# Three modulation vectors of layer 0: from GpSimd products with ScalarE row sums to TensorE products on four column groups

## The chip, the core and the metric

One core of a Trainium2 chip. The core has TensorE (PE in the rows; its weight loads are PEld), VectorE (DVE), ScalarE (ACT), GpSimd (POOL) and SyncE (SP), which issues nearly all DMAs. Each engine works off its own queue in order and waits on semaphores for the others. The metric is the device time of one execution in microseconds (us); lower is better.

## The reference, cut to what matters

Two layers of a backbone over 512 tokens (256 of context, 256 latent) of 1024 features: layer 0 is a bidirectional Mamba-2 mixer and a SwiGLU feed-forward, layer 1 a bidirectional RWKV-7 mixer and a mixture of experts. Both are modulated by vectors made from a conditioning vector, `c` for the latent tokens and `c_ctx` for the context:

```python
m  = split(silu(c)     @ mod_w[i] + mod_b[i], 6)
mc = split(silu(c_ctx) @ mod_w[i] + mod_b[i], 6)
h  = rmsnorm(x, norm1_g[i]) * (1 + m[1]) + m[0]
x  = x + m[2] * mixer(h)
h2 = rmsnorm(x, norm2_g[i]) * (1 + m[4]) + m[3]
x  = x + m[5] * ffn(h2)
```

So each layer has six parts, each a product of a 1024 x 1024 matrix with two vectors. Parts 0 and 1 of layer 0 are wanted first, part 2 at the end of its mixer, parts 4 and 3 at its second norm, part 5 in its feed-forward. All is float32.

## The kernel before, in words

The activations lie feature-major, 128 features on the partitions and 512 tokens along a row. A large product takes a weight tile of 1024 x 256 in two loads of 512 KB (`wraw`, L190 to L198, from a ring of five tiles), which ScalarE rounds to a leading part (`whi`, L206) and VectorE, or GpSimd for the tiles of z, subtracts to a trailing part (`wlo`, L207). TensorE then does three matmuls per block (L212 to L214) into accumulator banks (`acc`, three of them; `misc`, two, is for everything small).

There are two ways to make a modulation vector.

`mod_products(n)` (L236) makes 256 entries of it, two feature tiles, and is used for parts 0 and 1 in the prologue (n from 0 to 7, L350). It loads a 1024 x 256 tile of `mod_w`, clears an accumulator bank on VectorE (L240), and for each of the 8 blocks of 128 rows multiplies by the 2 columns of silu(c) with the 2 columns as the weights and 256 columns as the moving data (L243). Block k goes to partitions 32 (k mod 4), so that four column groups of the array each sum two blocks. ScalarE copies the bank to SBUF (`modev`, L245), two matmuls with a 0/1 matrix `sel` add the four groups up and turn them onto the partitions (L248), and VectorE adds the bias (L250).

`mod_sums(l, part, js, eng)` (L253) makes one feature tile of 128 entries per step from the transposed weights: it loads 512 KB, multiplies them by a broadcast silu(c) (`scb`) and takes the row sums. Where `eng` is VectorE, a product and its row sum are one instruction (L261), one for each of the two vectors. Where it is GpSimd, GpSimd multiplies (L264) into `mprod`, of which there is one, or in place, and ScalarE copies the product over itself with a row sum (L265). Eight steps make a part, and VectorE adds the bias at the next call (L269).

`mod_queue` (L272) strings the parts together, layer 0's 2, 4, 3 (GpSimd and ScalarE) and 5 (VectorE), then layer 1's six (VectorE): 80 steps. `mod_some(n)` (L275) takes the next n steps. It is called at the head of a weight product: two steps in `x_products` (L491, 8 calls), one in `gate_z` (L573, 8 calls), so that parts 2, 4 and 3 are done by the end of the mixer; two at each of the four output products (L615); none in the first four feed-forward tiles, two in most others (L648, L661); what is left goes ahead of the RWKV part (L679).

The mixer of layer 0 runs over four groups of heads, each in two halves. `inputs` makes B and C, `x_products` the projection of x, `mix` convolves (`conv`: four tap sums per tile, L459), builds chunk states (GpSimd's products L520, matmuls L523) and per head a decay mask by exponentials on ScalarE (L546), multiplied by C times B on VectorE (L548) and by x on TensorE (L551). `gate_z` projects z and gates, with a running sum of squares on GpSimd (L303). Before it stands a chain of small VectorE operations on the time steps (L404 to L440), which ends in transposes on TensorE (L439).

The order on each queue isn't the program's: it is planned at build time by a list scheduler with its own estimates of durations, which takes the instructions by their place in the program and fills gaps with later ones. On the chip each queue then keeps that order.

Of the kernel before, what the change touches and what calls it, by code (L numbers as in the profile page):

```python
# [10 lines left out]
F32 = mybir.dt.float32  # L11
# [3 lines left out]
AF = mybir.ActivationFunctionType  # L15
# [50 lines left out]
def prepare(inp):  # L66
# [4 lines left out]
    a["w_mod"] = _tiles(g["mod_w"][0], [[(256 * n, 256 * n + 256)] for n in range(8)])  # L71
# [47 lines left out]
    # of the even heads' products (0) the first rows, of the odd heads' (1) the last take the minus sign  # L119
# [18 lines left out]
def tile_backbone(ctx: ExitStack, tc: tile.TileContext, T, out: bass.AP, dbg=None, stop=99):  # L138
# [50 lines left out]
    def wraw(src):  # L189
        """one weight tile, four rows blocks at a time: the blocks' access patterns"""  # L190
        kt, n = src.shape[1], src.shape[2]
        out = []
        for k in range(0, kt, 4):
            m = min(4, kt - k)
            w = wp.tile([128, 4, 256], F32, name="wraw", bufs=5)
            SY.dma_start(w[:, :m, :n], src[:, k:k + m, :])
            out.append(w[:, :m, :n])
        return out  # L198
# [17 lines left out]
    def accumulate(o, w, x_at, k0, nk):  # L216
        """add the products of the weight tile's row blocks k0, k0 + 1, ... of nk; four blocks for one
        column tile at a time, so that the next bank is asked for late"""
        c = o[0].shape[0]
        for q in range(0, len(w), 8):  # L220
            for m in range(len(o)):
                for i, (hi, lo) in enumerate(w[q:q + 8]):
                    k = k0 + q + i
                    mm3(o[m], hi[:, c * m:c * m + c], lo[:, c * m:c * m + c], *x_at(k), k == 0, k == nk - 1)

# [10 lines left out]
    def mod_products(n):  # L236
        """the first two parts of layer 0, wanted first: products of the tensor engine"""
# [6 lines left out]
        ev = xp.tile([128, 256], F32, name="modev", bufs=2)  # L244
# [8 lines left out]
    def mod_sums(l, part, js, eng):  # L253
        """the other parts: row sums of the transposed weights times silu(c)"""
        for n in range(8 * part, 8 * part + 8):
            w = wp.tile([128, 4, 256], F32, name="wraw", bufs=5).rearrange("p a b -> p (a b)")
            SY.dma_start(w, T["w_modT"][l, n])
            for j in js:
                t = w if j == js[-1] else rowp.tile([128, D], F32, name="mprod", bufs=1)
                if eng is V:  # L260
                    V.scalar_tensor_tensor(t, w, 0.5, scb[:, j, :], op0=ALU.mult, op1=ALU.mult,  # L261
                                           accum_out=mods[l][:, n, j:j + 1])
                else:
                    G.tensor_mul(t, w, scb[:, j, :])  # L264
                    S.activation(t, t, AF.Copy, scale=0.5, accum_out=mods[l][:, n, j:j + 1])  # L265
# [5 lines left out]
    MOD_ENG = {(0, 2): G, (0, 4): G, (0, 3): G, (0, 5): V}  # L271
    mod_queue = (x for l, part in ((0, 2), (0, 4), (0, 3), (0, 5), (1, 1), (1, 0), (1, 2), (1, 4), (1, 3), (1, 5))  # L272
                 for x in mod_sums(l, part, (0, 1) if l == 0 or part < 2 else (0,), MOD_ENG.get((l, part), V)))

# [7 lines left out]
    # token halves: ctx columns 0..255 take modulation 1, latent columns 256..511 modulation 0  # L282
    HALF = ((slice(0, 256), 1), (slice(256, 512), 0))

    class Squares:
        """running sum of squares over feature tiles, and from it 1/rms of each token on every partition"""
# [5 lines left out]
        def add(self, src, late=False):  # L292
            """late: summed by the tensor engine, with the rows"""
# [30 lines left out]
    def norm_mod(pool, l, norm, rb, X, hi, lo):  # L324
        """adaLN: hi + lo = X * rb * g * (1 + scale) + shift"""
# [31 lines left out]
    # =====================================================================  # L357
    # layer 0 mixer: bidirectional Mamba-2
    # =====================================================================
# [4 lines left out]
    with ExitStack() as es:  # L364
# [11 lines left out]
        def project(w, n=2, cols=128):  # L376
            """products of n column tiles of a weight tile"""
# [5 lines left out]
        # -- time steps: softplus, decay sums in both directions  # L383
# [23 lines left out]
        # log1p(e) = 2 atanh(e / (2 + e)), series in the square of the quotient (at most 1/9)  # L407
# [41 lines left out]
        def conv(o, m, dst):  # L449
            """centred depthwise convolution of one feature tile, per sequence, and silu;  # L450
            half the convolution is taken, h, and silu(2 h) = h (tanh(h) + 1)"""
# [18 lines left out]
        def inputs(g):  # L470
            """the group's B and C, feature-major; B token-major; products of C and B in each chunk"""
# [18 lines left out]
        def x_products(g, s):  # L490
            mod_some(2)  # L491
            return project(wsplit(T["w_mb"][5 * g + 1 + 2 * s], XE))

        def mix(g, s, px, bf, cf, btm, cb):
            """convolution, states and sums of four heads in both directions"""
# [16 lines left out]
            # states entering each chunk  # L512
# [59 lines left out]
        def gate_z(g, s):  # L572
            mod_some(1)  # L573
# [28 lines left out]
    # gated norm and output projection; the norm's factor is applied after the product  # L602
# [29 lines left out]
    # =====================================================================  # L632
    mark("ffn")
    # layer 0 feed-forward: SwiGLU, its hidden features in two halves
    # =====================================================================
    with ExitStack() as es:
# [8 lines left out]
        for hf in range(2):  # L645
            hid = []
            for n in range(NH):
                mod_some(0 if hf == 0 and n < 4 else 2)  # L648
# [26 lines left out]
    # =====================================================================  # L675
    # layer 1 mixer: bidirectional RWKV-7, in chunks of 64 tokens
    # =====================================================================
# [14 lines left out]
    # a block's rows of its second and of its first half  # L692
# [12 lines left out]
    # sigmoid(z) = (1 + tanh(z / 2)) / 2, and 1 + (sigmoid(z) - 1) k_a likewise  # L705
# [7 lines left out]
    # states of each direction, and the solutions of a chunk: the even heads' tile holds zeros in  # L713
    # the odd heads' rows and the other way round
# [5 lines left out]
    def weave(*gens):  # L720
        """emit the pieces of several instruction streams in turn"""
# [16 lines left out]
    def later(dst, src, after):  # L738
        """a load that leaves the queue to the transfers before after is there"""
# [3 lines left out]
    class Weights:  # L743
        """weight tiles in the order of their use: loaded ahead by halves, split by pairs of row blocks"""

        def __init__(self, pool, srcs, nraw, nsp, after=None, eng=(V, G), raw=None, part=None, first=SY):
            """raw, part: where the weights and their parts wait, when not in pool"""
# [36 lines left out]
    def products(W, units, x_at, nk=8):  # L784
        """units of nk feature tiles each: (columns, token-major, done). Both column tiles of a unit
        share a bank. x_at(unit, k) gives the two parts of the unit's k-th feature tile"""
# [24 lines left out]
    def normed(up, j):  # L811
        """modulated norm of one token sequence (0: ctx, 1: latent), feature-major, a zero at either end"""
        mj = 1 - j
        # each tile of the latent stream gives way to the difference of its neighbours
# [16 lines left out]
    def unit_keys(F, hT, rs, kbank):  # L831
        """the keys times the reciprocal of each head's norm, rs"""
# [7 lines left out]
    def features(up, F, names, MB, nraw, nsp, base, normed_all=None, vx=None, xs=None, later_x=None, raw=None, part=None, tail=None, eng=(V, G)):  # L840
        """projections of one sequence, feature-major except the values"""
# [75 lines left out]
        def value(n):  # L917
            def done(o):
                # rows of the head's opposite half
# [31 lines left out]
        def x_at(u, k):  # L951
# [4 lines left out]
            # the next mixture's tile takes the place of the last but one  # L956
# [17 lines left out]
    class Unit:  # L974
        """half of the heads of one token sequence (0: ctx, 1: latent), both directions"""
# [14 lines left out]
    def stage(tp, rp, F, un, d, l2, nb, bks, tags, ready):  # L990
        """everything of one direction of a unit that needs no state, but for the inverses"""
# [54 lines left out]
        def operands(c, dd, slot):  # L1046
# [6 lines left out]
            # the even heads' tile holds zeros in the odd heads' rows and the other way round  # L1053
# [12 lines left out]
        def grams(c, BK, slot):  # L1066
            """products of the earlier tokens (rows) with the later (columns), masked"""
# [44 lines left out]
    def spin(o, x):  # L1112
        """products that nothing reads, between the short ones: the tensor engine's clock falls to half when it waits"""
        PE.matmul(o[:, :x.shape[1] * x.shape[2]], ident, x, start=True, stop=True)

    def invert(tp, un, zbank, slots={}, warm=(0, 0)):
        """inverses of the unit triangular blocks: by substitution in 16 by 16 blocks, two per partition,
        then joined by products, first in blocks of 32, then of 64. In between blocks on the partitions
        turn into rows on the partitions. Of the second direction the substitution sees the transposes.
        slots: the tiles to take the place of, with their shapes; warm: after how many columns spin runs,  # L1120
        in either set of products"""
# [16 lines left out]
        # the diagonal 32 by 32 blocks; the chunks that are last in either direction come last  # L1138
# [9 lines left out]
        # of a block's upper triangle the rows of its first and of its second half  # L1148
# [8 lines left out]
        for n in range(16):  # L1157
            # column n is final: its multiples go to the columns after it; in the first half also to the
            # other half's columns, which become the inverse's product with the off-diagonal block
# [11 lines left out]
        # the inverses of one direction and the transposes of the other's share a tile  # L1171
# [8 lines left out]
        # minus that product, its other half on the partitions  # L1180
# [34 lines left out]
        for d in range(2):  # L1215
# [13 lines left out]
            # no products from the later half to the earlier  # L1229
# [4 lines left out]
    def scan(F, un, y=None):  # L1234
        """both directions of a unit through their chunks"""
# [61 lines left out]
    class Places:  # L1297
        """a pool some of whose tiles are another's"""
# [576 lines left out]
```

## Time and profile before

| | us |
|---|---|
| median of 3 runs (2755.1 to 2763.13) | 2755.29 |
| span of the profiled execution, first to last instruction | 2756.0 |
| prologue and first norm of layer 0 (to about) | 47 |
| layer 0 mixer, with the time steps | 47 to 545 |
| output product, second norm, feed-forward | 545 to 1000 |
| layer 1 | 1000 to 2756 |

One execution was recorded by the profiler. The page shows no time around its span; the span is 0.7 us above the median of the runs. In the rows an instruction is named by the line of the kernel, engine, operation, and output<-inputs by tile names. A group's row ends with its count, its busy us, the mean ns of one, and the idle time of the engine before it with what ended that. The bounds of the stages in the table are read from the lines that run there; the planned order overlaps neighbours by some us.

### The profile page before, as it was taken

Reading aid. Unit: us, or ns where it says so; the run is one execution under the profiler, and the core shown is the slowest. Engines: PE = TensorE matmul, PEld = TensorE weight load, DVE = VectorE, ACT = ScalarE, POOL = GpSimd, SP = SyncE. Lnnn points to the kernel's source line nnn. Section 1 sums busy time; section 2 is a strip of 40 time slices with the busy share of each in tenths; the row PEclk is TensorE's granted clock in tenths of the full one; section 3 lists DMA queues with packets and bytes.
Section 4 is the critical chain, followed back from the end, with each engine's and each line's share of the span. In section 5 each row is a group of like instructions: output and inputs, shape, how many; then the busy total and the mean of one; then the engine's idle time right before and its main releaser. Section 6 shows DMA issues by size and latency. Waiting matters only on the chain. (4 is left out here: it accounts for less than half of the span.)

```text
span 2756.0 us, 42800 instructions
## 1 busy us (share of the span) xinstructions
PE 2503.4 (91%) x16570; PEld 2049.0 (74%) x16570; DVE 2157.6 (78%) x3097; ACT 1500.6 (54%) x2374; POOL 552.1 (20%) x554
## 2 busy tenths in 40 slices
PE   7699988899999988787987889899999999999997
PEld 4567666687888877676877768788788788878875
DVE  6897878846755367768876764799899989999997
ACT  4454554523222235433533423677787878777775
POOL 4554443210000045423363412000000000000001
PEclk9899999999999988668798969899999999999999
DMA  7222221233556332002201015599899989989994
GB/s 259 100 78 76 77 84 47 77 123 115 187 185 200 117 129 68 17 15 70 81 17 63 2 57 214 192 366 360 327 364 361 362 331 369 357 337 365 370 339 169
DMA packets 99203, 511.49 MB, mean 186 GB/s; under 512 B 11648, under 2 KB 19072, under 8 KB 55216
## 3 DMA queue, kind: packets, MB, share of 16 engines
q1 hardware_dynamic: 97520, 506.52, 50.5%
q8 instruction: 132, 2.16, 0.3%
q10 hardware_dynamic: 1472, 2.16, 0.3%
q14 instruction: 79, 0.65, 0.1%
HBM read 506.54 MB, written 2.10 MB: 185 GB/s over the span
## 5 line engine op out<-in xcount | busy, mean ns | idle before, releaser
L1732 DVE TENSOR_TENSOR wlo<-wraw,whi 128x1024 fp32r<-128x1024 f32 x662 | 798.1, 1224 | 68.8 <-ACT whi L1731 48.5
L1731 ACT CAST whi<-wraw 128x1024 fp32r<-128x1024 f32 x662 | 694.4, 1051 | 206.5 <-PE gu L214 112.3
L213 PE MATMUL gu<-wlo,xg 128*128 128x512 f32 x896 | 355.6, 397 | 1.5 <-DVE wlo L1732 0.7
L214 PE MATMUL gu<-whi,xg 128*128 128x512 f32 x896 | 350.2, 391 | 0.0
L212 PE MATMUL gu<-whi,xg 128*128 128x512 f32 x896 | 336.8, 392 | 1.1 <-ACT xg L1751 0.9
L206 ACT CAST whi<-wraw 128x1024 fp32r<-128x1024 f32 (+2 forms) x126 | 129.6, 1028 | 224.8 <-PE acc L213 220.8
L207 DVE TENSOR_TENSOR wlo<-wraw,whi 128x1024 fp32r<-128x1024 f32 (+2 forms) x110 | 142.4, 1295 | 105.3 <-ACT whi L206 102.3
L1806 POOL TENSOR_TENSOR wraw<-yx,SH 128x512 f32<-128x512 f32 x4 | 7.4, 1860 | 1022.3 <-DVE yx L1802 1022.3
L213 PEld LDWEIGHTS gu<-wlo,xg 128*128 128x128 f32 x896 | 168.7, 188 | 42.4 <-DVE wlo L1732 5.8
L212 PEld LDWEIGHTS gu<-whi,xg 128*128 128x128 f32 x896 | 168.7, 188 | 38.2 <-ACT xg L1751 1.6
L214 PEld LDWEIGHTS gu<-whi,xg 128*128 128x128 f32 x896 | 168.9, 188 | 31.6
L213 PE MATMUL y<-wlo,HT 128*128 128x512 f32 x448 | 178.1, 398 | 2.3 <-DVE wlo L1732 2.1
L212 PE MATMUL y<-whi,HT 128*128 128x512 f32 x448 | 175.9, 394 | 3.0 <-DVE xg L1752 3.0
L214 PE MATMUL y<-whi,HT 128*128 128x512 f32 x448 | 175.8, 392 | 0.0
L214 PE MATMUL acc<-hhi,wlo 128*128 128x512 f32 (+1 forms) x328 | 137.6, 421 | 10.2 <-DVE wlo L207 10.2
L212 PE MATMUL acc<-hhi,whi 128*128 128x512 f32 (+1 forms) x328 | 139.8, 426 | 3.5 <-ACT cv L455 2.2
L212 PE MATMUL acc<-h2hi,whi 128*128 128x512 f32 x352 | 137.5, 394 | 3.4 <-ACT h2hi L341 3.4
L303 POOL TENSOR_TENSOR sqa<-sqa,sq 128x512 f32<-128x512 f32 (+1 forms) x35 | 47.2, 1349 | 462.6 <-issue 311.1
L213 PE MATMUL acc<-hlo,whi 128*128 128x512 f32 (+1 forms) x328 | 137.2, 418 | 2.4 <-DVE cv L454 2.4
L213 PE MATMUL acc<-h2lo,whi 128*128 128x512 f32 x352 | 137.9, 392 | 0.0
L214 PE MATMUL acc<-h2hi,wlo 128*128 128x512 f32 x352 | 134.8, 392 | 0.0
L775 POOL TENSOR_TENSOR wlo<-wraw,whi 128x512 fp32r<-128x512 f32 (+1 forms) x69 | 86.5, 1263 | 146.7 <-ACT whi L774 139.9
(581 smaller groups left out, 5811.5 us busy)
## 6 DMA issues: line engine op xcount, KB each, us to landing
wraw<-in_w_mi_dram SPq DMA_DIRECT2D x219, 1024.0 KB, 4.9
wraw<-in_w_mo_dram SPq DMA_DIRECT2D x112, 1024.0 KB, 4.9
wraw<-in_w_modT_dram SPq DMA_DIRECT2D x80, 512.0 KB, 3.5
wraw<-in_w_ffi_dram SPq DMA_DIRECT2D x44, 512.0 KB, 3.8
wraw<-in_w_mb_dram SPq DMA_DIRECT2D x40, 512.0 KB, 3.4
wraw<-in_w_mod_dram SPq DMA_DIRECT2D x16, 512.0 KB, 6.8
wraw<-in_w_mbo_dram SPq DMA_DIRECT2D x16, 512.0 KB, 3.5
wraw<-in_w_ffo_dram SPq DMA_DIRECT2D x16, 512.0 KB, 3.6
```

Of the source, the lines that this page charges most:

```text
L206: S.copy(hi, raw)
L207: eng[q % len(eng)].tensor_sub(lo, raw, hi.bitcast(F32))
L212: PE.matmul(o, whi, xhi, start=start, stop=False)
L213: PE.matmul(o, whi, xlo, start=False, stop=False)
L214: PE.matmul(o, wlo, xhi, start=False, stop=stop)
L303: G.tensor_add(self.acc, self.acc, sq)
L775: self.eng[self.n % len(self.eng)].tensor_sub(lo, raw, hi.bitcast(F32))
L1731: S.copy(hi, raw[:, k:k + 2, :])
L1732: V.tensor_sub(lo, raw[:, k:k + 2, :], hi.bitcast(F32))
L1806: G.tensor_mul(xf[:, tt, 512 * n:512 * n + 512], fs, fg[:, 512 * n:512 * n + 512])
```

## The change

Parts 2, 4 and 3 of layer 0 are made by `mod_products` (n from 8 to 19, twelve calls, as steps of the queue in that order) and no longer by `mod_sums` on GpSimd and ScalarE (24 steps). Part 5 and layer 1 stay on VectorE. `mod_some` is called for fewer steps in the mixer: one in `x_products`, one in the first four calls of `gate_z`, none in the others: 12 in all. The first four tiles of the feed-forward take one step each, so that nothing is left for the call ahead of the RWKV part. The weights of the three parts come from `w_mod` and not from `w_modT`. `modev` moves to a pool that lives longer. Removed comments are not shown.

```diff
-    a["w_mod"] = _tiles(g["mod_w"][0], [[(256 * n, 256 * n + 256)] for n in range(8)])
+    a["w_mod"] = _tiles(g["mod_w"][0], [[(256 * n, 256 * n + 256)] for n in range(20)])
...
-        ev = xp.tile([128, 256], F32, name="modev", bufs=2)
+        ev = rowp.tile([128, 256], F32, name="modev", bufs=2)
...
-    def mod_sums(l, part, js, eng):
+    def mod_sums(l, part, js):
...
-                if eng is V:
-                    V.scalar_tensor_tensor(t, w, 0.5, scb[:, j, :], op0=ALU.mult, op1=ALU.mult,
-                                           accum_out=mods[l][:, n, j:j + 1])
-                else:
-                    G.tensor_mul(t, w, scb[:, j, :])
-                    S.activation(t, t, AF.Copy, scale=0.5, accum_out=mods[l][:, n, j:j + 1])
+                V.scalar_tensor_tensor(t, w, 0.5, scb[:, j, :], op0=ALU.mult, op1=ALU.mult,
+                                       accum_out=mods[l][:, n, j:j + 1])
...
-    MOD_ENG = {(0, 2): G, (0, 4): G, (0, 3): G, (0, 5): V}
-    mod_queue = (x for l, part in ((0, 2), (0, 4), (0, 3), (0, 5), (1, 1), (1, 0), (1, 2), (1, 4), (1, 3), (1, 5))
-                 for x in mod_sums(l, part, (0, 1) if l == 0 or part < 2 else (0,), MOD_ENG.get((l, part), V)))
+    def mod_parts(*parts):
+        for part in parts:
+            for n in range(4 * part, 4 * part + 4):
+                mod_products(n)
+                yield
+
+    mod_queue = chain(mod_parts(2, 4, 3), (
+        x for l, part in ((0, 5), (1, 1), (1, 0), (1, 2), (1, 4), (1, 3), (1, 5))
+        for x in mod_sums(l, part, (0, 1) if l == 0 or part < 2 else (0,))))
...
         def x_products(g, s):
-            mod_some(2)
+            mod_some(1)
...
         def gate_z(g, s):
-            mod_some(1)
+            mod_some(1 if g < 2 else 0)
...
-                mod_some(0 if hf == 0 and n < 4 else 2)
+                mod_some(1 if hf == 0 and n < 4 else 2)
```

## Rows read from the trace of the kernel before

**Rows 1.** The page, part 1: busy time, share of the span, instructions, per engine.
```profile
PE 2503.4 (91%) x16570; PEld 2049.0 (74%) x16570; DVE 2157.6 (78%) x3097; ACT 1500.6 (54%) x2374; POOL 552.1 (20%) x554
```
**Rows 2.** Stretches: length; busy us (instructions) of PE, PEld, DVE, ACT, POOL; clock; DMA.
```profile
47.00:545.00 498.00, 426.70 (x2090) 321.13 (x2089) 424.26 (x580) 252.88 (x564) 230.42 (x127) 0.93 0.24 81
...
100.00:120.00 20.00, 9.32 (x34) 7.26 (x34) 19.59 (x28) 8.50 (x14) 9.95 (x5) 0.69 0.31 105
...
200.00:300.00 100.00, 91.19 (x454) 69.69 (x454) 81.11 (x111) 50.17 (x112) 45.16 (x26) 0.95 0.24 79
300.00:400.00 100.00, 89.85 (x445) 67.36 (x445) 78.51 (x108) 52.55 (x115) 51.34 (x30) 0.98 0.24 80
...
580.00:600.00 20.00, 20.00 (x90) 16.57 (x89) 11.49 (x19) 4.80 (x6) 2.97 (x2) 1.00 0.39 136
```
**Rows 3.** VectorE by form, 47 to 545 us: count, busy us, mean ns, idle.
```profile
L459 DVE SCALAR_TENSOR_TENSOR cy<-cv,cwh,cy 128x512 f32<-128x512 f32 x96 | 98.8, 1036 | 0.8
L548 DVE TENSOR_TENSOR W<-E,cb 128x512 f32<-128x512 f32 x64 | 60.2, 949 | 8.6 <-ACT E L546 6.7 <-PE py L551 1.6
L207 DVE TENSOR_TENSOR wlo<-wraw,whi 128x1024 fp32r<-128x1024 f32 x27 | 44.2, 1639 | 6.9 <-ACT whi L206 3.8 <-PE acc L212 2.1 <-issue 0.8
```
**Rows 4.** Single lines, 47 to 545 us: count, ns min/median/max, first and last start.
```profile
L459 DVE SCALAR_TENSOR_TENSOR cy<-cv,cwh,cy x96: 735/745/2878, 65.8 to 460.9; 128x512 f32<-128x512 f32 x96
...
L548 DVE TENSOR_TENSOR W<-E,cb x64: 677/684/2897, 135.1 to 533.6; 128x512 f32<-128x512 f32 x64
...
L207 DVE TENSOR_TENSOR wlo<-wraw,whi x27: 1205/1225/3407, 47.1 to 525.3; 128x1024 fp32r<-128x1024 f32 x27
...
L509 DVE TENSOR_TENSOR xdt<-misc,dtTM x32: 674/680/692, 133.9 to 500.2; 128x512 f32<-128x512 f32 x32
```
**Rows 5.** Groups by form, 47 to 545 us, GpSimd (POOL) and ScalarE (ACT).
```profile
L264 POOL TENSOR_TENSOR wraw<-wraw,scb 128x1024 f32<-128x1024 f32 x24 | 63.7, 2656 | 1.4
L264 POOL TENSOR_TENSOR mprod<-wraw,scb 128x1024 f32<-128x1024 f32 x24 | 63.5, 2645 | 60.1 <-DMA wraw<-in_w_modT_dram 47.7 <-ACT mprod L265 7.2 <-ACT xs L579 5.1
L265 ACT ACTIVATE mprod<-mprod 128x1024 f32<-128x1024 f32 x24 | 25.6, 1066 | 34.2 <-POOL mprod L264 34.2
L265 ACT ACTIVATE wraw<-wraw 128x1024 f32<-128x1024 f32 x24 | 25.4, 1059 | 9.8 <-POOL wraw L264 9.8
```
**Rows 6.** Waits, 47 to 545 us: who waited for whom, total us, times, longest.
```profile
ACT mprod L265 <- POOL mprod L264: 34.2, 12, 6.0
PE py L551 <- DVE W L548: 15.5, 12, 4.7
PE misc L439 <- DVE cp L435: 10.9, 1, 10.9
PE acc L214 <- DVE wlo L207: 10.2, 3, 5.0
```
**Rows 7.** Timeline of the prologue: start, length, instruction; last, line 243 alone.
```profile
16.76 3.55 PE L311 MATMUL misc<-cst,sq 128*128 128x1 f32 x16
20.24 2.74 PE L243 MATMUL acc<-wraw,cc 128*2 128x256 f32 x24
22.91 1.11 PE L320 MATMUL misc<-cst,rst 128*128 128x128 f32 x4
24.39 0.27 DVE L240 MEMSET acc<- 128x256 f32 x1
32.32 0.37 ACT L245 COPY modev<-acc 128x256 f32<-128x256 f32 x1 [3.43 <-PE acc L243]
36.35 1.01 PE L248 MATMUL misc<-cst,modev 128*128 128x2 f32 x4 [0.78 <-ACT modev L245]
41.52 1.03 PE L243 MATMUL acc<-wraw,cc 128*2 128x256 f32 x8
43.81 1.18 PEld L248 LDWEIGHTS misc<-cst,modev 128*128 128x128 f32 x4 [0.20 <-issue]
...
L243 PE MATMUL acc<-wraw,cc x128: 582/631/634, 12.2 to 41.9; 128*2 128x256 f32 x128
```

## The prediction

> **What bounds the kernel now.** I read the engines' shares of the whole first. TensorE is busy 91% of a span of 2756.0 us and VectorE 78% [rows 1]: an average over stages with different limits, so it says nothing yet about this change. The second view, stretches of time, does. The stage in which the removed work runs lies between 47 and 545 us (time steps, convolutions and states of the layer 0 mixer). There TensorE is busy 426.7 of 498 us at a granted clock of 0.93, VectorE 424.3, ScalarE 252.9, GpSimd 230.4 [rows 2]. Two engines at 85% each, neither saturated: they take turns waiting. In the feed-forward behind it, TensorE is busy 20.00 of 20 us at clock 1.00 [rows 2]: there it alone is the bound, and VectorE has 8 us of 20 free.
>
> The third view explains VectorE's 85%. By form, its tap sums of the convolution (line 459) average 1036 ns, its mask products (L548) 949, its weight splits (L207) 1639 [rows 3]; the single-line view gives medians of 745, 684 and 1225, with maxima of 2878, 2897 and 3407 [rows 4]. The maxima lie about 2.2 us over the median: most of a GpSimd product of 2.65 us [rows 5], waited out. L509, which reads PSUM, has a maximum of 692 on a median of 680 [rows 4]: it is not touched. So VectorE work with both inputs in SBUF stalls behind GpSimd, and the removed products (L264) are 127.2 us of GpSimd's time there [rows 5].
>
> The fourth view, the waits, says who feels it. Of TensorE's 498 - 426.7 = 71.3 us idle, the three largest waits, 15.5, 10.9 and 10.2 us, are for VectorE [rows 6]. ScalarE stands 34.2 us in front of a row sum until GpSimd's product is there [rows 6], with all that is queued behind it.
>
> **The change, part by part.**
> *GpSimd's products go (48).* VectorE's excess over its medians is 96 x 0.291 = 28.0 us (L459), 64 x 0.265 = 17.0 (L548), 27 x 0.414 = 11.2 (L207), together 56 us on 203 us of busy time [rows 3, 4]. L264 is 127.2 of the 230.4 us that GpSimd is busy there, 55% [rows 2, 5]. Lower end for what VectorE gets back: 0.55 x 56 = 31 us. Upper end, if all of its 424 us were stretched alike (56/203 = 28%): 0.55 x 117 = 64 us. I take 55, near the upper end, since only operations reading PSUM are exempt. Late next, once GpSimd is emptier: its own split of the z weights (L207), which stays and waits for ScalarE.
>
> *ScalarE's row sums go (48).* 25.6 + 25.4 us of ACTIVATE [rows 5], with accumulator reads about 60, and the 34.2 us wait. ScalarE is half idle, so I count this as nothing by itself; its worth is that exponentials and weight casts behind it start earlier. If TensorE proves to wait on ScalarE, it is worth up to the 34.
>
> *TensorE's products come (12).* Each is 8 fp32 matmuls on four column groups, recorded as 16, and 2 joining ones, recorded as 4. The prologue already does eight of them: 24 records take 2.74 us, so 16 take 1.83 [rows 7]; four joining records take 1.01 [rows 7]. With their edges I take 2.9 us, times 12 = 34.8 us of TensorE. Also 12 memsets of 0.27 us on VectorE and 12 additions to four columns, each shorter than that: between 3.2 and 6.5 us, and I take 5. On ScalarE 12 copies of 0.37, 4.4 us [rows 7].
>
> *The waits it adds.* TensorE's queue now holds a product that waits for a memset on VectorE, and a join that waits for ScalarE's copy; the next projection is queued behind both. Least: 0, if other matmuls stand between. Most: in the prologue the last product's matmuls end at 41.52 + 1.03 = 42.55 us and its join begins at 43.81 [rows 7], 1.3 us later, with ScalarE's copy in between, so 12 x 1.3 = 16 us. I take 0 and keep 16 for the range, since TensorE's queue here holds independent matmuls, and VectorE, which was late, has more room. Each product holds one of three accumulator banks and one of two small ones, for about 4 us; the projection takes two of three, and I count that under the same 16.
>
> *DMA.* A product loads two tiles of 512 KB where two steps loaded one each: the same bytes on SP's queue, in the same ring of five, at 24% DMA share [rows 2]. The cover is wide; without it a landing of some us would be seen 12 times. Costed at nothing.
>
> *Moved sums.* The queue is 12 steps shorter in the mixer and 4 steps of layer 1 go from the stage's end (before the RWKV part) into the first feed-forward tiles. There TensorE is full and VectorE has room [rows 2]: nothing.
>
> *Sum.* VectorE falls to 424.3 - 55 + 5 = 374 us. TensorE rises to 426.7 + 34.8 = 461.5 us: it becomes the bound of the stage. Its clock of 0.93 is a mean over the two levels, 2.4 and 1.2 GHz. The lower one goes with idleness here: from 100 to 120 us, where TensorE is busy 9.3 of 20 us, the mean is 0.69, and from 300 to 400 us it is 0.98 [rows 2]; with VectorE less late I take 0.97, that is 0.04 x 498 x 0.86 = 17 us of busy time back: 444.5. Then its share. Now it is 85.7%, in its best 100 us 91.2% [rows 2] with VectorE at 81%; after the change VectorE is at 77%, so I take 92%. 444.5 / 0.92 = 483 us in place of 498: **15 us gained**, 2756.0 - 15 = 2741. The profiled execution stands 0.7 us above the median of 2755.29 of the runs, so I forecast 2740.
>
> Whether TensorE can enter and leave column groups free of charge shows in the prologue: the record of 128x128 matmuls that starts at 16.76 ends at 20.31, the column-grouped ones start at 20.24 and end at 22.98, the next full-width ones start at 22.91 [rows 7]. No gap. The Trainium skill, "TensorEngine Tiling (Array Packing)", section Tiling Modes, says otherwise: changing the tiling mode drains TensorE. This is the third rival below.
>
> **The rivals.**
> *More is gained.* If VectorE's lateness was nearly all of the idle time, TensorE reaches 96%: 444.5 / 0.96 = 463, 35 us gained, 2720. For it: the three largest waits are on VectorE [rows 6]. Against: TensorE's best 100 us reached only 91%. Chance 0.18.
>
> *Nothing moves.* TensorE's share stays near its best stretch of today, 89.5%, with the regained clock: 444.5 / 0.895 = 497, 2754. For it: from 300 to 400 us TensorE is idle 10% at a clock of 0.98 already [rows 2], so its remaining idle time is not all stalls of VectorE. Chance 0.12.
>
> *Column groups drain.* The same forecast, less one drain at each of the two changes of mode per product. A drain costs at most what a matmul lasts, 0.63 us in the records of the grouped products (their pitch is far shorter, 2.74 us for 24 [rows 7]): 24 x 0.63 = 15 us, 2755. Against: no gap in the prologue. Chance 0.08. The rule of the Trainium skill named above is this mechanism; in it the trace so far does not agree.
>
> *Slower.* TensorE's in-order queue. The twelve products sit ahead of the weight products of the same call; if each join stands on ScalarE's copy as in the prologue, the added work is 34.8 + 16 = 51 us, and no clock returns since TensorE still idles: 426.7 + 51 = 477.5, at 93% (the waits are in the sum now) 513, **15 us lost**, 2770. It decides where less than about 36 us of the 71 idle are filled. For it: TensorE has only 9 to 10 us idle per 100 between 200 and 400 us [rows 2], and it is there that the queue of the mixer calls for most products. Against: the same stretches lose VectorE's stalls. Chance 0.20, in which I also put that the four column groups run one after the other (16 x 0.63 = 10 us per product, 121 in all); the 2.74 us for 24 records speak against that.
>
> **How the numbers follow.** The forecast has 0.42. A measurement of this kernel tells about 0.3% (8 us) from no change. Faster by more: forecast and larger gain, 0.60. Within: 0.12 + 0.08 = 0.20. Slower: 0.20. The range goes from 2712 (the larger gain, with the upper end of 64 us for VectorE) to 2770 (most of the slower case); the tails left out are about 0.07 below and 0.10 above.
>
> **What would show it.** Right: L459 and L548 average under 900 ns; GpSimd's busy time falls by about 127 us; TensorE's share in the stage is above 90% and its clock above 0.95; the mixer ends near 530 us instead of 545; from there on the two traces run in parallel. Wrong: TensorE idle before the joining matmuls with ScalarE's copy as releaser, or before the first grouped matmul with the memset; a gap at each change between grouped and full-width matmuls; VectorE's averages unchanged because the remaining GpSimd work meets it instead; or a difference that arises only after 1000 us, where this change has no work.

## The result and the profile after

The changed kernel takes 2694.14 us (median of 4 runs, 2689.01 to 2704.16) against 2755.34 (4 runs, 2755.1 to 2763.13): a ratio of 0.9774, 95% interval 0.9749 to 0.9798, 61 us faster. I had forecast 2740 and a range from 2712 to 2770. The sign was right and the size was not: the gain is four times the 15 us of the forecast, and above the 35 us of the rival *more is gained*. The profiled execution has a span of 2702.3 us; it is the longest of the four runs.

The end of the mixer can be read from one line, the gating of z on VectorE, which runs 16 times. These are its rows in the kernel before (line 583) and after (L585), with count, ns min/median/max, first and last start:

```profile
L583 DVE SCALAR_TENSOR_TENSOR yz<-xs,yz x16: 676/686/2761, 167.7 to 537.8; 128x512 f32<-128x512 f32 x16
```
```profile
L585 DVE SCALAR_TENSOR_TENSOR yz<-xs,yz x16: 679/686/1103, 129.2 to 477.2; 128x512 f32<-128x512 f32 x16
```

The last gate starts at 477.2 us and not at 537.8: the mixer ends 60.6 us earlier. The first gate is already 38 us early; in front of it stands the chain on the time steps, where VectorE was busy 19.59 of 20 us [rows 2]. What follows the mixer nearly keeps its length: by the medians the kernel gains 61.2 us, as much as the mixer. The profiled span is only 53.7 us shorter, since that execution is the longest of the four, 10 us over their median; the 7 us in between lie behind the mixer.

The stage of [rows 2], 47 to 545 us, is now 47 to 486, and the 455 us behind it are the output product and feed-forward as before. Stretches of the kernel after: length, busy us (instructions) of PE, PEld, DVE, ACT, POOL, then TensorE's clock, DMA share, GB/s.

```profile
47.00:486.00 439.00, 426.06 (x2335) 320.03 (x2334) 344.57 (x605) 210.62 (x483) 101.18 (x79) 0.99 0.27 93
...
486.00:941.00 455.00, 448.63 (x1979) 370.65 (x1979) 254.48 (x367) 131.10 (x161) 21.26 (x23) 0.99 0.45 149
...
200.00:300.00 100.00, 100.00 (x573) 77.31 (x573) 78.02 (x140) 49.85 (x119) 25.29 (x21) 1.00 0.24 85
300.00:400.00 100.00, 99.14 (x523) 73.80 (x522) 80.28 (x126) 42.49 (x92) 27.87 (x20) 1.00 0.27 90
```

TensorE is busy for the same 426 us as before [rows 2], now in 439 us in place of 498: 97%, at a clock of 0.99 in place of 0.93. Between 200 and 400 us it stands idle for 0.9 us. GpSimd fell from 230.4 to 101.2 us, VectorE from 424.3 to 344.6.

Single lines of VectorE in the kernel after, 47 to 486 us (the tap sums and mask products are lines 461 and 550 now), and their groups, the last for GpSimd's own splits:

```profile
L461 DVE SCALAR_TENSOR_TENSOR cy<-cv,cwh,cy x96: 653/748/2944, 59.4 to 401.5; 128x512 f32<-128x512 f32 x96
...
L550 DVE TENSOR_TENSOR W<-E,cb x64: 664/685/1778, 98.0 to 472.7; 128x512 f32<-128x512 f32 x64
...
L207 DVE TENSOR_TENSOR wlo<-wraw,whi x27: 1207/1220/1636, 47.4 to 466.2; 128x1024 fp32r<-128x1024 f32 x27
```
```profile
L461 DVE SCALAR_TENSOR_TENSOR cy<-cv,cwh,cy 128x512 f32<-128x512 f32 x96 | 85.5, 892 | 1.1
L550 DVE TENSOR_TENSOR W<-E,cb 128x512 f32<-128x512 f32 x64 | 45.9, 727 | 14.9 <-ACT cb L489 5.6 <-ACT E L548 4.6 <-PE py L553 4.1
L207 DVE TENSOR_TENSOR wlo<-wraw,whi 128x1024 fp32r<-128x1024 f32 x27 | 33.7, 1247 | 9.0 <-ACT whi L206 9.0
L207 POOL TENSOR_TENSOR wlo<-wraw,whi 128x1024 fp32r<-128x1024 f32 x16 | 41.6, 2603 | 90.3 <-ACT whi L206 90.3
```

The medians are those of [rows 4]; the means fell from 1036 to 892 and from 949 to 727 ns. What is left above the medians goes for the most part with GpSimd's own splits of the z weights (L207, 41.6 us): with these on VectorE, in the last experiment, the tap sums average 784 ns. The waits of TensorE changed most. In the kernel after, 47 to 486 us (waiter, releaser, total us, times, longest):

```profile
PE acc L212 <- ACT yhi L610: 4.4, 1, 4.4
PE misc L568 <- DVE st L533: 2.9, 2, 2.5
PE misc L441 <- DVE cp L437: 1.6, 1, 1.6
PE py L553 <- DVE xdt L511: 1.3, 2, 0.9
```

Where three waits for VectorE took 36.6 us [rows 6], the largest is 4.4 us, for ScalarE at the start of the next stage.

### The profile page after: what moved, and what is told of

The parts are those of the page before. It is cut to its first block, busy times and chain, and to the rows that moved or that the text cites. A ratio compares the mean times of both kernels' runs of the same rounds, so it can differ in the third digit from the quotient of the medians.

```text
span 2702.3 us, 43164 instructions
## 1 busy us (share of the span) xinstructions
PE 2499.3 (92%) x16810; PEld 2043.9 (76%) x16810; DVE 2070.4 (77%) x3118; ACT 1455.4 (54%) x2290; POOL 416.1 (15%) x506
## 5 line engine op out<-in xcount | busy, mean ns | idle before, releaser
L207 DVE TENSOR_TENSOR wlo<-wraw,whi 128x1024 fp32r<-128x1024 f32 (+2 forms) x110 | 131.7, 1198 | 106.3 <-ACT whi L206 106.2
```

The lines of the kernel that those rows point to most:

```text
L207: eng[q % len(eng)].tensor_sub(lo, raw, hi.bitcast(F32))
```

## The experiments

Two main theories stood after the result. **Theory 1:** VectorE, held up by GpSimd's products, was what the mixer waited for. **Theory 2:** it was ScalarE, with 60 us of row sums and its wait for GpSimd in its queue. And open was what TensorE pays. That TensorE waited for results of GpSimd itself was a third, and the trace of the kernel before speaks against it: of TensorE's waits in the stage, those for GpSimd come to 4.1 us, in this line.

```profile
PE misc L523 <- POOL xw L520: 4.1, 2, 3.8
```

The kernel before ran beside each group of kernels, with medians of 2754.5 to 2756.0; each ratio is to those runs. "Slower than the changed kernel" is a difference to 2694.14 us, measured in a group of its own, and runs of one kernel lie up to 23 us apart. So the last gate's start is given as well where it matters: 537.8 us in the kernel before, 477.2 in the changed one, each from one execution.

**GpSimd's products left out, row sums kept**

```diff
-                    G.tensor_mul(t, w, scb[:, j, :])
-                    S.activation(t, t, AF.Copy, scale=0.5, accum_out=mods[l][:, n, j:j + 1])
+                    S.activation(t, w, AF.Copy, scale=0.5, accum_out=mods[l][:, n, j:j + 1])
```

> The kernel before with GpSimd's 48 products left out and ScalarE's 48 row sums kept (they sum the raw weights). Theory 1, the loss was VectorE standing behind GpSimd: nearly all is gained, 60 to 75 us, 2680 to 2695. Theory 2, the loss was ScalarE's 60 us of sums and their place in its queue: only the 34 us of waiting for GpSimd can come back in part, 10 to 25 us, 2730 to 2745.

Measured 2701.47 us, ratio 0.9809 (0.979 to 0.9827), 54.5 us faster: 6 us short of what theory 1 expected, far from theory 2. The last gate starts at 475.5 us.

**Row sums left out, GpSimd's products kept**

```diff
+    V.memset(mods[0][:, 16:40, :], 0.0)
...
-                    S.activation(t, t, AF.Copy, scale=0.5, accum_out=mods[l][:, n, j:j + 1])
```

> The kernel before with GpSimd's 48 products kept and ScalarE's 48 row sums left out (parts 2, 4 and 3 of layer 0 are zero plus bias). Theory 1: VectorE's line averages stay near 1036 and 949 ns and little is gained, 0 to 20 us, 2735 to 2755. Theory 2: 40 to 60 us, 2695 to 2715.

Measured 2750.42 us, ratio 0.9968 (0.9951 to 0.9986), 5.6 us faster, as theory 1 expected. The last gate starts at 528.2 us.

The mixer of both as a stretch: first without the products, then without the row sums.

```profile
47.00:484.00 437.00, 406.71 (x2082) 311.55 (x2081) 344.46 (x574) 251.84 (x561) 103.97 (x79) 0.97 0.27 91
```
```profile
47.00:537.00 490.00, 417.55 (x2094) 318.73 (x2093) 428.05 (x581) 206.25 (x471) 227.13 (x127) 0.94 0.25 82
```

Without the products, VectorE is busy 344 us, as in the changed kernel, though ScalarE still does all its sums (252 us, as before). Without the sums, VectorE stays at 428 us and the mixer at 490. That shows theory 1, and refutes theory 2 as the main cause.

**Both left out**

```diff
+    V.memset(mods[0][:, 16:40, :], 0.0)
...
-                t = w if j == js[-1] else rowp.tile([128, D], F32, name="mprod", bufs=1)
+                t = w if j == js[-1] or eng is G else rowp.tile([128, D], F32, name="mprod", bufs=1)
...
-                    G.tensor_mul(t, w, scb[:, j, :])
-                    S.activation(t, t, AF.Copy, scale=0.5, accum_out=mods[l][:, n, j:j + 1])
+                    pass
```

> The kernel before with GpSimd's 48 products and ScalarE's 48 row sums left out; the loads stay, parts 2, 4 and 3 of layer 0 are zero plus bias. It gives what the removal alone is worth, without TensorE's new work. If the mixer is now bound by TensorE, the 12 products of some 1.5 us each at the full clock (16 records in 1.04 us and 4 joining ones in 0.5, in the trace of the changed kernel) cost their 18 us, and this comes out near 2676 us. If they lie in idle time, it equals the changed kernel, 2694.

Measured 2690.06 us, ratio 0.9756 (0.9735 to 0.9777). Its gate line and its mixer:

```profile
L583 DVE SCALAR_TENSOR_TENSOR yz<-xs,yz x16: 677/687/1249, 130.8 to 467.5; 128x512 f32<-128x512 f32 x16
```
```profile
47.00:476.00 429.00, 404.95 (x2093) 311.45 (x2092) 344.19 (x579) 205.00 (x470) 102.32 (x79) 0.98 0.28 94
```

By its total this kernel can't be told from the changed one: the medians differ by 4 us, and the runs overlap. By the mixer the truth lies between the two expected values. The mixer ends 9.7 us before that of the changed kernel, by the gate line (467.5 against 477.2), while TensorE is busy 426.1 - 405.0 = 21 us less. So the twelve products put 21 us on TensorE, and half of it lay in time that TensorE stood idle anyway. And with GpSimd out of the way, ScalarE's sums do cost something: 2701.47 - 2690.06 = 11 us.

**GpSimd's work put back into the changed kernel**, in three forms: whole products, products in halves, copies. Nobody reads them.

```diff
                 mod_products(n)
+                for j in range(4):
+                    G.tensor_mul(rowp.tile([128, D], F32, name="mprod", bufs=1), scb[:, 0, :], scb[:, 1, :])
                 yield
```

> The changed kernel with 48 GpSimd products of 128x1024 put back, four at each TensorE product, of two tiles that are there anyway; nobody reads them and there are no row sums. Theory 1: VectorE's stalls of some 60 us return, TensorE has only 13 us of idle time in the mixer to lose, so 35 to 60 us are lost, 2730 to 2755. Theory 2: under 10 us.

Measured 2761.22 us, ratio 1.003 (1.0017 to 1.0043): 67 us slower than the changed kernel: all of its gain, and 7 us more than theory 1 gave it at most. The last gate starts at 544.8 us. TensorE's waits for VectorE in the mixer add up to 55 us in the kernel before, 7 in the changed one, and 52 here.

```diff
+                for j in range(8):
+                    G.tensor_mul(rowp.tile([128, D], F32, name="mprod", bufs=1)[:, :512], scb[:, 0, :512], scb[:, 1, :512])
```

> The changed kernel with 96 GpSimd products of 128x512 in place of the 48 of 128x1024 put back before: about the same busy time in shorter pieces. If VectorE waits out the GpSimd operation that it meets, the longest of VectorE's line 461 falls from about 2.9 to 2.0 us and there are more of them; the total loss stays between half and all of the 67 us, 2728 to 2761. If the loss goes by the number of operations, it is 2761 or more.

Measured 2755.27 us, ratio 0.9997 (0.9979 to 1.0016): 61 us slower than the changed kernel. The last gate starts at 526.7 us.

```diff
+                for j in range(4):
+                    G.tensor_copy(rowp.tile([128, D], F32, name="mprod", bufs=1), scb[:, 0, :])
```

> The changed kernel with 48 GpSimd copies of 128x1024 beside the TensorE products: one input in place of the two of the products put back before (which cost 67 us). If any GpSimd work holds VectorE up for as long as it lasts, the loss goes by GpSimd's busy time: a copy that lasts half of the 2.65 us loses about half, 25 to 40 us. If only a second input does it, under 10 us.

Measured 2720.5 us, ratio 0.9871 (0.9842 to 0.9899): 26 us slower than the changed kernel. The last gate starts at 491.5 us.

The groups of GpSimd's added work and of the tap sums on VectorE (both shifted by two lines), for whole products, halves and copies. (The first few of the added operations run ahead of the stretch and are not counted.)

```profile
L463 DVE SCALAR_TENSOR_TENSOR cy<-cv,cwh,cy 128x512 f32<-128x512 f32 x96 | 114.4, 1196 | 1.2
L272 POOL TENSOR_TENSOR mprod<-scb 128x1024 f32<-128x1024 f32 x43 | 113.7, 2644 | 2.4
```
```profile
L272 POOL TENSOR_TENSOR mprod<-scb 128x512 f32<-128x512 f32 x87 | 137.0, 1574 | 5.6
L463 DVE SCALAR_TENSOR_TENSOR cy<-cv,cwh,cy 128x512 f32<-128x512 f32 x96 | 110.0, 1149 | 1.2
```
```profile
L463 DVE SCALAR_TENSOR_TENSOR cy<-cv,cwh,cy 128x512 f32<-128x512 f32 x96 | 91.6, 959 | 0.8
L272 POOL COPY mprod<-scb 128x1024 f32<-128x1024 f32 x43 | 55.7, 1294 | 1.4
```

All three hold VectorE up, but not by one rate. For 114, 137 and 56 us of it the totals lose 67, 61 and 26 us; the mixer alone, by its last gate, loses 68, 50 and 14. That is between a quarter and six tenths of GpSimd's time. A single input doesn't spare VectorE; that copies cost less for each of their us than products may lie in the one input or in their shorter time, which these runs don't separate. Cutting the products into pieces gives a little back, 6 us of the total and 18 of the mixer, although a piece lasts longer than half of a whole (1574 of 2644 ns). One part of what I had expected of the halves fell: the longest tap sum did not shrink to 2.0 us (it is 2922 ns), which the remaining whole-width splits of L207 may cause.

**The twelve products on one column group**

```diff
-            q = 32 * (k % 4)
-            PE.matmul(pm[q:q + 2, :256], cc[:, k, :], w[k], start=k < 4, stop=k >= 4)
+            q = 0 if n >= 8 else 32 * (k % 4)
+            PE.matmul(pm[q:q + 2, :256], cc[:, k, :], w[k], start=k == 0 if n >= 8 else k < 4, stop=k == 7 if n >= 8 else k >= 4)
```

> The changed kernel with its 12 new products on one column group: all 8 blocks add up on the same two partitions, one after the other. At the full clock 16 records of 256 columns then take about 3.4 us in place of 1.04 (estimate: half of a 512-column record's pitch of 0.23 us is 0.11, times two for float32). If TensorE is the bound of the mixer, 12 x 2.4 = 29 us are lost, 2723; if its time there is still covered, 0 to 5, 2694 to 2699.

Measured 2718.58 us, ratio 0.9854 (0.9816 to 0.9892): 24 us slower than the changed kernel. The group of the product's matmuls in the mixer, first in the changed kernel, then here:

```profile
L243 PE MATMUL acc<-wraw,cc 128*2 128x256 f32 x192 | 18.4, 378 | 0.0
```
```profile
L243 PE MATMUL acc<-wraw,cc 128*2 128x256 f32 x192 | 45.5, 379 | 0.0
```

Records of the same length, 27 us more of busy time: on four groups they run beside each other, on one they queue. Of these 27 us 20 reach the mixer's last gate (497.3 us) and 24 the end. So TensorE is now the bound of the mixer for most of the work that is added to it.

**VectorE in place of TensorE**: all three parts (in the kernel before), or part 3 alone (in the changed kernel, once with its sums called for in the mixer, once in the output product).

```diff
-    MOD_ENG = {(0, 2): G, (0, 4): G, (0, 3): G, (0, 5): V}
+    MOD_ENG = {(0, 2): V, (0, 4): V, (0, 3): V, (0, 5): V}
```

> The kernel before with parts 2, 4 and 3 as product and row sum in one VectorE instruction, 48 of them of 1.22 us, 59 us. Theory 1: VectorE trades about 65 us of stalls for 59 us of work and is busy over 90% of the mixer, so that only part comes back: 15 to 45 us, 2710 to 2740. Theory 2: ScalarE is free of the sums and GpSimd's wait, nearly all comes back, 2690 to 2700.

Measured 2707.62 us, ratio 0.9835 (0.981 to 0.9861). Its mixer:

```profile
47.00:505.00 458.00, 414.72 (x2089) 317.75 (x2088) 398.80 (x676) 203.54 (x467) 104.26 (x79) 0.95 0.26 88
```

48 us gained, a little more than theory 1 gave it: VectorE is busy 399 us in place of 424 with 59 us of new work in it, so even work costs it less than the stalls did. But it is at 87% of its stage again, TensorE's clock at 0.95, and the mixer is 19 us longer than with TensorE's products.

```diff
-    mod_queue = chain(mod_parts(2, 4, 3), (
-        x for l, part in ((0, 5), (1, 1), (1, 0), (1, 2), (1, 4), (1, 3), (1, 5))
+    mod_queue = chain(mod_parts(2, 4), (
+        x for l, part in ((0, 3), (0, 5), (1, 1), (1, 0), (1, 2), (1, 4), (1, 3), (1, 5))
...
-            mod_some(1 if g < 2 else 0)
+            mod_some(1)
```

> The changed kernel with part 3 on VectorE (16 instructions of 1.22 us, 20 us) and only parts 2 and 4 on TensorE: 8 products. If TensorE is the bound of the mixer and VectorE has its 94 us to spare there, 4 x 1.5 = 6 us are gained, 2688. If VectorE's lateness still decides in places, 0 to 10 us are lost.

Measured 2705.92 us, ratio 0.982 (0.9794 to 0.9846), 12 us slower than the changed kernel, a little more than the 10 that I gave it. Its last gate starts at 486.2 us, 9 us later, and TensorE's largest wait in the mixer is for VectorE again:

```profile
PE py L553 <- DVE W L550: 9.4, 4, 6.3
```

So VectorE still decides in places, and here four products on TensorE are cheaper than sixteen sums on VectorE.

```diff
-            mod_some(1 if g < 2 else 0)
+            mod_some(0)
...
-            mod_some(2)
+            mod_some(3 if n == 3 else 2)
...
-                mod_some(1 if hf == 0 and n < 4 else 2)
+                mod_some(2)
```

> A try at a faster version: parts 2 and 4 as TensorE products in the mixer, part 3 as VectorE sums called for in the output product, where TensorE is full and VectorE has a third to spare, part 5 and the rest one place later. The mixer loses a third of the products, worth 3 us by the 10 us that the mixer ends earlier without any; if the planner draws the sums forward into the mixer, as with part 3 there, it loses up to 12 us. 2691, or 2694 to 2706.

(These lines are changed beside the two of the queue above.) Measured 2707.79 us, ratio 0.9819 (0.9792 to 0.9847). Its gate line:

```profile
L585 DVE SCALAR_TENSOR_TENSOR yz<-xs,yz x16: 679/689/1104, 134.4 to 473.8; 128x512 f32<-128x512 f32 x16
```

The mixer does end 3.4 us earlier, as expected, and yet the median is 14 us above that of the changed kernel and above both of my figures, though the runs of the two (2698.09 to 2712.82, 2689.01 to 2704.16) overlap. In the profiled executions 8 us are lost behind the mixer; why, is not shown. I didn't find a faster version this way.

**The z weights' trailing parts on VectorE**

```diff
-        XE, ZE = (V,), (G,)
+        XE, ZE = (V,), (V,)
```

> The changed kernel with the 16 trailing parts of the z weights made by VectorE, not by GpSimd. VectorE gets 16 x 1.22 = 19.5 us of work and loses the 20 us or so of stalls that line 207 on GpSimd still gives it. Theory 1: even, and with TensorE at 97% no difference beyond 5 us, 2689 to 2699. If stalls cost TensorE more than even work does, faster by up to the 13 us that it is idle.

Measured 2698.21 us, ratio 0.9796 (0.9769 to 0.9822): no difference from the changed kernel that can be told. Its mixer and its tap sums:

```profile
47.00:485.00 438.00, 424.46 (x2333) 319.15 (x2332) 340.71 (x620) 209.83 (x481) 61.84 (x63) 0.98 0.27 92
...
L461 DVE SCALAR_TENSOR_TENSOR cy<-cv,cwh,cy 128x512 f32<-128x512 f32 x96 | 74.8, 784 | 0.8
```

VectorE has 19.5 us of work more and is busy 4 us less, so stalls of some 23 us were traded for that work.

## Why the prediction was wrong in size

**The mechanism held.** VectorE stood behind GpSimd's products; with them gone it came down from 424 to 345 us, and leaving the products out alone gives 54.5 of the 61 us. My 55 us for what VectorE gets back was too low: 424.3 - 344.6 is 80, although the shorter stretch holds 25 instructions more (605 against 580), 5 us of new work among them. The three lines that I summed gave back 98.8 - 85.5 = 13.3 us (tap sums), 60.2 - 45.9 = 14.3 (mask products) and 44.2 - 33.7 = 10.5 (weight splits), 38 together; the rest came from lines that I hadn't counted. That two engines at 85% each can hide one that is the cause was right as well.

**The term that failed first: the price of a product, 2.9 us.** I took it from the prologue [rows 7], the only place where the trace of before shows these matmuls. There TensorE's matmuls take the time of the lower of its two levels, 1.2 GHz. The stretch view and TensorE's timeline of the kernel before, up to 60 us:

```profile
0.00:40.00 40.00, 25.73 (x172) 14.26 (x172) 18.42 (x44) 16.42 (x28) 10.49 (x10) 1.00 0.86 314
58.00:60.00 2.00, 2.00 (x6) 1.52 (x6) 2.00 (x3) 2.00 (x3) 0.37 (x1) 0.52 0.00 0
```
```profile
48.82 0.63 PE L214 MATMUL acc<-hhi,wlo 128*64 128x512 f32 x1
49.25 0.60 PE L212 MATMUL acc<-hhi,whi 128*64 128x512 f32 x1
49.68 0.40 PE L213 MATMUL acc<-hlo,whi 128*64 128x512 f32 x1
49.92 0.40 PE L214 MATMUL acc<-hhi,wlo 128*64 128x512 f32 x1
...
58.55 0.63 PE L213 MATMUL acc<-hlo,whi 128*128 128x512 f32 x1
58.98 0.63 PE L214 MATMUL acc<-hhi,wlo 128*128 128x512 f32 x1
```

Between 58 and 60 us the granted clock is 0.52, about the lower level, and there a matmul over 512 columns lasts 0.63 us, with starts 0.43 us apart. The same shape takes just that up to 49 us, and 0.40 us, with starts 0.24 apart, behind it. The stretch view lists 1.00 for the first 40 us, but the trace holds no record of the clock before 49.69 us, where the first one begins, at full speed; the durations show what the column can't. In the mixer of the kernel after, at the higher level, one product and its join look like this:

```profile
201.39 1.05 PE L487 MATMUL misc<-cf,bf 128*128 128x128 f32 x8
202.37 1.04 PE L243 MATMUL acc<-wraw,cc 128*2 128x256 f32 x16
203.35 0.39 PE L542 MATMUL pbc<-parts,ehb 96*128 96x512 bf16 x1
203.58 0.38 PE L543 MATMUL pbc<-maskb,identb 128*128 128x512 bf16 x1
203.80 0.50 PE L248 MATMUL misc<-cst,modev 128*128 128x2 f32 x4
```

1.04 us for the 16 records and 0.50 for the join, against 1.83 and 1.01. By the groups, products and joins are 18.4 + 6.3 = 25 us of the mixer; by the kernel without them, 21. I had 34.8. Twelve times this example would be 18.5 us: only four of the twelve products run in one piece like it. The plan splits the others, 24 pieces in all, and a piece of two records lasts 0.59 us, nearly as long as one of eight (0.61). And I gave the clock back only up to 0.97, 17 us, where it came to 0.99: without any products TensorE was busy 405.0 us, 22 less than before. Together that makes TensorE's 426 us in place of my 444.5, worth 444.5/0.92 - 426/0.92 = 20 of the 44 us by which the stage was missed.

**The term that failed second: TensorE's share, 92%.** I drew it from the best 100 us of the kernel before, 91.2%. But those were as full of VectorE's stalls as the others: between 200 and 400 us the tap sums average 1007 ns. At 426 us of work, the step from 92 to 97% is 463 - 439 = 24 us, the other half of the miss. I should have asked what TensorE waited for in those best stretches, too (between 200 and 400 us its largest wait is 10.4 us, for VectorE's mask products); the kernel with both parts left out reaches 94.4% without any new work to fill gaps with, and the products then fill half of what is left.

**The waits I added.** I took 0 and kept 16 us for the range. The 16 was misread: in the prologue the row at 43.81 us is the join's weight load, and TensorE is at work on the next projection from 43.33 on. It was 0: in the timeline above, matmuls of the heads stand between the product and its join, while ScalarE copies, and none of TensorE's larger waits in the mixer names the copy or the memset.

**The rivals.** *More is gained* had the share nearly right, 96% where 97% came, and fell short by the price: 426 us at its 96% would be 444, where 439 were measured. *Slower* needed joins that stall, and there are none. *Column groups drain* had the mechanism right, and my "no gap" was misread. I compared ends with starts, but records overlap (0.39 us long, starts 0.23 apart), so an end hides a gap and only starts show it. Two pieces of products in the kernel after, with their neighbours:

```profile
63.18 0.39 PE L213 MATMUL acc<-hlo,whi 128*128 128x512 f32 x1
63.41 0.39 PE L214 MATMUL acc<-hhi,wlo 128*128 128x512 f32 x1
63.73 1.04 PE L243 MATMUL acc<-wraw,cc 128*2 128x256 f32 x16
64.70 0.50 PE L212 MATMUL acc<-hhi,whi 128*128 128x512 f32 x1
```
```profile
223.02 0.61 PE L243 MATMUL acc<-wraw,cc 128*2 128x256 f32 x8
223.56 0.70 PE L525 MATMUL misc<-xw,btm 128*128 128x256 f32 x2
```

The way into the groups takes 0.32 us from start to start where full-width matmuls take 0.23, so 0.09 us more. On the way out, sixteen records take 0.97 us to the next start and eight take 0.54; the difference, 0.43, is what eight cost, so 0.11 us more pass. The Trainium skill, "TensorEngine Tiling (Array Packing)", section Tiling Modes, has changes of mode drain TensorE; this trace agrees, at about 0.1 us a change. The rival's price was at most 0.63 us for each of 24 changes, 15 us; the 24 pieces make 48 changes, some 5 us (an estimate, 48 x 0.1), which are part of the 21 to 25 us above.

**GpSimd's hold on VectorE** is on a page, too. The Trainium skill, "GPSIMD Engine Reference", section Specifications, says that GpSimd shares its SBUF interfaces with VectorE, in contention with VectorE instructions that run in a 2-port mode or have two SBUF inputs. The traces agree in which instructions are hit (L459 up to 2878 ns, L509 with a PSUM input never over 692 [rows 4]) and add the price: between a quarter and six tenths of GpSimd's busy time in the three forms tried.

## What to carry to other kernels

Where VectorE is one of two engines near 85%, look at the maximum of its commonest lines beside the median: if it exceeds the median by a GpSimd operation, GpSimd's share of the page is not free, and its elementwise work is worth moving even onto an engine that looks as busy. Before a price is carried from one stage into another, compare a matmul of known shape in both stages: a clock of half speed shows in its duration even where the clock column doesn't show it. Read gaps between matmuls from their starts, not from their ends. And a share read from a kernel whose bound is about to be removed is no ceiling for the kernel after.

## What was not expected of the hardware

Behind the mixer all kernels here are nearly the same apart from the order in which their instructions are planned, yet that part is not equally long: from the last gate to the end it takes 2208 us in the kernel with all sums on VectorE and 2232 in the one with halves of GpSimd's products. Two stretches of 350 us of layer 1, from about 453 us behind the last gate on, for the former, then for the latter:

```profile
949.00:1299.00 350.00, 273.68 (x3202) 238.47 (x3202) 254.57 (x561) 163.12 (x398) 144.55 (x214) 0.78 0.17 54
1299.00:1649.00 350.00, 297.88 (x4466) 257.60 (x4465) 249.31 (x556) 132.22 (x336) 128.65 (x179) 0.86 0.14 48
```
```profile
981.00:1331.00 350.00, 278.85 (x3199) 243.03 (x3197) 252.52 (x559) 162.46 (x398) 142.56 (x212) 0.75 0.17 54
1331.00:1681.00 350.00, 296.20 (x4242) 254.90 (x4242) 239.76 (x531) 128.20 (x324) 130.02 (x179) 0.81 0.13 43
```

The mean clock is 0.78 and 0.86 in one, 0.75 and 0.81 in the other. In the changed kernel it is 0.78 and 0.83, with part 3 called for late 0.76 and 0.82. That this makes the spread between the runs of one kernel, or what part 3 called for late lost behind its mixer, is likely and not shown. Whether the order of the instructions or the moment of the run decides the clock there was not tried.
